# Where list tiles, best entries' rows, the squares of x and the batched heads' selection stand in a fused decoder block

## The chip, the cores and the metric

The kernel runs on one core of one Trainium2 chip. Its time is the device time of one execution, in microseconds (us). The core has five engines that work side by side and each take their own instructions in order: TensorE (PE: matmuls, with its weight loads listed as PEld), VectorE (DVE), ScalarE (ACT), GpSimd (POOL), and SyncE (SP), which here only issues DMA transfers. PE alone has a clock that a throttle grants in part or in full. Transfers between HBM and the on-chip memory run on 16 DMA engines that all queues share.

## The reference

One decoder layer over 1024 tokens of width 1024, all in float32:

```python
h = modulate(rms_norm(x, norm1_w), shift1, scale1)
proj = h @ w_in          # q k v r a_lr su sv g_a g_b
o_gla = rms_norm(gla_chunked(q, k, v, log_a)) * silu(r)
o_sgu = gelu(su) * (W_s @ layer_norm(gelu(sv)) + b)
x = x + gate1 * ((sigmoid(g_a) * o_gla + sigmoid(g_b) * o_sgu) @ w_out)
h2 = modulate(rms_norm(x, norm2_w), shift2, scale2)
x = x + gate2 * peer(h2)
out = rms_norm(x, final_norm_w)
```

`gla_chunked` is gated linear attention with 4 heads. `peer` is a mixer of 16384 one-neuron experts with 8 heads: each token's query of a head is scored against two sets of 128 keys, the 16 best of each set are combined, the 16 best sums name 16 experts, and the output is the sum over heads and experts of softmax weight x gelu(h2 . down[e]) x up[e], where down and up are rows of 1024 numbers. The shifts, scales and gates come from a conditioning vector c.

## The kernel before

**Layout of the work.** The tokens go in two halves of 512 (hf = 0, 1), each of four blocks of 128. For a half the projections are made in weight groups of 512 columns: V0, V1, QK0, QK1, SV0, SV1, R0, R1, A0, A1, SU0, SU1, B0, B1 of w_in, then two passes of w_out, then the four query groups of peer_w_q (w_q; group 0 in two parts of two blocks). A group runs through `stream` (L1264): eight steps k = 0 to 7, one per 128 rows of the weight, each with twelve matmuls of 512 columns into four PSUM accumulators (tag mm, four buffers). Matmuls are made exact by splitting both operands into a high and a low half (fp32r): `weights_ahead` (L1246) loads a weight tile on SP, ACT makes the high half wh (L1253), DVE the low half wl (L1254), three steps ahead, with four tiles staged. After the eighth step the four accumulators are evicted (`evac`), and the next group's first matmul needs the first of them free.

**What runs beside the groups.** At the end of each step `step()` (L1045) pumps generators, which each trace a little more work and yield. A queue has a credit: pump(n) adds n, and one turn is taken for each whole unit. The queues are: qa, the conditioning rows; qr, the routing of the experts; qm, the norms; qf, finishing blocks; qp, the expert stream `peer_stream` (L779); qdir, `direct_rows` (L739). Rates are 1.0 for qr, RP = RP2 = 0.84 for qp (RP3 = 1.3 in the last three query groups of the second half) and RD = 0.62 for qdir.

**Experts.** For each head the best entry (the first of the 16) is known early, by token, and is called a best entry's row: `direct_rows` treats 4 blocks x 8 heads = 32 of them in the second half. For each it gathers 128 rows of down and 128 of up (L752, POOL), takes the dot with h2 on DVE (L764), gelu on ACT (L766), a weight (L767) and adds the up rows times the weight (L773, or L769 on ACT for a block's first head). The gelu is held behind the gates' logarithms (`zlast`). The other entries are packed into list tiles of 128 (token, expert) pairs: `entry_list` (L542) picks indices with a one-hot matmul (L548, L549), gathers both rows at once (L525), `entry_dot` (L572) brings the tokens' h2 rows by matmul into an accumulator (L578, L579), which DVE reads for the dot (L580), or takes gathered h2 rows (L585); the up rows are split (L617 on ACT, L618 on DVE) and added by matmul (L625, L626). List tiles run in the second half from group SV0 on, and then alone after the last query group. Heads that may need more than eight of one key set are batched: `rare` (L390) finds them, gathers their scores (qsc, L428) and selects 16 of each set with `tops16` (L203), then packs them (`pack_rare`). For the first half (gi = 0) it stands in qr after that half's routing, so its turns come in the second half's first groups.

**Order on the engines.** The kernel is written in one program order, but a planner that replays it with its own estimates of durations fixes each engine's order: of the operations that it holds ready, the earlier in the program goes first. Waits between engines are made from the data. `issue_after(ins)` puts an operation behind a given one on the same engine. A generator's place in the program is thus a priority, not a time. On the chip each engine then keeps that order, and an operation that waits holds all behind it.

**The places that the change touches.** `x_prep` (L1170), called after the first half's query group 1 (L1679), loads four tiles of x (xb, tag b4, eight buffers), squares them on ACT with a sum (L1176), makes the reciprocal norms, spreads them over partitions by a matmul (L1165) into an accumulator of the pool aux (two buffers, used by the scores too) and a copy (rrow, L1167), loads xT in four tiles (L1182) and multiplies them (L1184); `h_split` (L1209) later makes hTh and hTl of the second half from it. `ev_qk` (L1366) evicts the QK groups with DVE operations L1382 to L1384 for q and L1399 to L1402 for k. `gla_head` (L1406) runs one head of the attention over four pairs of chunks p, and pumps qdir in each. `w_q` (L1602) evicts a query group on ACT (qt, L1607); `s_part` (L1648) then makes the scores (L1655), copies them (so, L1657) and finds the top 8 (L200, L201).

## Time and profile before

| | |
|---|---|
| median of 3 runs | 1451.9 us (1449.78 to 1454.23) |
| the profiled execution's own time | 1450.17 us |
| its span, first to last instruction | 1448.4 us |
| mean granted PE clock | 0.971 |
| PE busy | 1348.1 us, 93% |
| PE weight loads busy | 1039.6 us, 72% |
| DVE busy | 1091.7 us, 75% |
| ACT busy | 737.9 us, 51% |
| POOL busy | 278.7 us, 19% |
| moved by DMA | 345 MB, mean 238 GB/s |

In the span the first half's groups run from about 34 to 577 us, the second half's from there to about 1245, and the remaining list tiles to the end. A row of a timeline gives start, duration, engine, line, operation, tiles (out<-in), shapes and count, and in brackets the engine's idle time before it with what ended that. A row of waits gives total, count and longest. A row of the chain of waits gives start, duration and what the chain went through. Rows of windows give the stretch, its length and each engine's busy time with its count, then PE's granted clock, the DMA engines' share and GB/s. L12 is line 12 of the kernel.

### The profile page before, as it was taken

Reading aid. Unit: us, or ns where it says so; the run is one execution under the profiler, and the core shown is the slowest. Engines: PE = TensorE matmul, PEld = TensorE weight load, DVE = VectorE, ACT = ScalarE, POOL = GpSimd, SP = SyncE. Lnnn points to the kernel's source line nnn. Section 1 sums busy time; section 2 is a strip of 40 time slices with the busy share of each in tenths; the row PEclk is TensorE's granted clock in tenths of the full one; section 3 lists DMA queues with packets and bytes.
Section 4 is the critical chain, followed back from the end, with each engine's and each line's share of the span. In section 5 each row is a group of like instructions: output and inputs, shape, how many; then the busy total and the mean of one; then the engine's idle time right before and its main releaser. Section 6 shows DMA issues by size and latency. Waiting matters only on the chain.

```text
span 1448.4 us, 19642 instructions
## 1 busy us (share of the span) xinstructions
PE 1348.1 (93%) x6004; PEld 1039.6 (72%) x6004; DVE 1091.7 (75%) x3114; ACT 737.9 (51%) x1611; POOL 278.7 (19%) x275
## 2 busy tenths in 40 slices
PE   3999999999999889997989999999988999789996
PEld 2778877888888778776868787887766886445553
DVE  6584768443468669988879888778889877799775
ACT  4454333333255456474534677556645555556542
POOL 0100001000000011422442133221111024443331
PEclk8899999999999999998999999999998999999999
DMA  9552454322258484757587689796687669987984
GB/s 321 184 214 95 170 184 161 105 95 88 88 171 280 160 291 168 265 177 275 194 308 263 222 325 343 286 354 216 219 324 264 227 216 356 355 347 303 419 331 166
DMA packets 120836, 345.00 MB, mean 238 GB/s; under 512 B 15033, under 2 KB 24505, under 8 KB 108690
## 3 DMA queue, kind: packets, MB, share of 16 engines
q0 software_dynamic: 32064, 165.95, 30.7%
q1 hardware_dynamic: 70992, 133.20, 26.8%
q10 hardware_dynamic: 17666, 44.53, 8.5%
q8 instruction: 48, 0.79, 0.2%
q14 instruction: 66, 0.54, 0.1%
HBM read 319.40 MB, written 24.23 MB: 237 GB/s over the span
## 4 chain that ended last, share of the span: by engine, by line
PE 41%; DMA 8%; DVE 7%; issue 5%; ACT 4%; POOL 1%; ACTq 0%; DVEq 0%; POOLq 0%
PE acc L606 7%; PE mm L181 6%; PE mm L182 6%; PE mm L184 6%; DMA uv<-in_tab_dram,ix 4%; PE mm L187 3%; PE mm L188 3%; PE mm L189 3%; PE aux L1655 2%; PE hps L578 1%; DMA wt<-in_w_inp_dram 1%; PE hps L579 1%; DVE wl L1254 1%; DVE uv L580 1%; DMA xb<-in_x_dram 1%
## 5 line engine op out<-in xcount | busy, mean ns | idle before, releaser
L1253 ACT ACTIVATE wh<-wt 128x512 fp32r<-128x512 f32 x368 | 228.2, 628 | 322.9 <-PE mm L182 133.5
L1254 DVE TENSOR_TENSOR wl<-wt,wh 128x512 fp32r<-128x512 f32 x368 | 247.7, 685 | 137.1 <-ACT wh L1253 73.2
L181 PE MATMUL mm<-wh,hTh 128*128 128x512 f32 x672 | 265.9, 398 | 3.1 <-ACT wh L1253 3.1
L182 PE MATMUL mm<-wh,hTl 128*128 128x512 f32 x672 | 263.8, 395 | 0.0
L184 PE MATMUL mm<-wl,hTh 128*128 128x512 f32 x672 | 207.6, 394 | 0.0
L181 PEld LDWEIGHTS mm<-wh,hTh 128*128 128x128 f32 x672 | 127.1, 189 | 35.0 <-ACT wh L1253 4.8
L182 PEld LDWEIGHTS mm<-wh,hTl 128*128 128x128 f32 x672 | 126.9, 189 | 27.1 <-issue 1.0
L184 PEld LDWEIGHTS mm<-wl,hTh 128*128 128x128 f32 x672 | 125.6, 188 | 27.0 <-DVE wl L1254 0.6
L525 POOL DMA_INDIRECT uv<-in_tab_dram,ix x74 | 80.4, 1086 | 262.9 <-ACT ix L557 178.3
L187 PE MATMUL mm<-wh,hTh 128*128 128x512 f32 x224 | 90.5, 413 | 8.4 <-ACT hTh L1211 5.5
L182 PE MATMUL mm<-hTl,wh 128*128 128x512 f32 x240 | 96.5, 402 | 0.0
L181 PE MATMUL mm<-hTh,wh 128*128 128x512 f32 x240 | 95.9, 400 | 0.0
L580 DVE SCALAR_TENSOR_TENSOR uv<-uv,hps 128x512 f32<-128x512 f32 x112 | 74.8, 679 | 24.5 <-DMA uv<-in_tab_dram,ix 16.8
L188 PE MATMUL mm<-wl,hTh 128*128 128x512 f32 x224 | 89.1, 398 | 0.1
L189 PE MATMUL mm<-wh,hTl 128*128 128x512 f32 x224 | 88.4, 397 | 0.0
L187 PE MATMUL mm<-hTh,wh 128*128 128x256 f32 (+1 forms) x208 | 71.6, 346 | 10.7 <-DVE q L1383 7.6
L188 PE MATMUL mm<-hTl,wh 128*128 128x256 f32 (+1 forms) x208 | 69.8, 337 | 3.0 <-DVE hTl L173 3.0
L184 PE MATMUL mm<-hTh,wl 128*128 128x512 f32 x240 | 71.4, 398 | 0.0
L752 POOL DMA_INDIRECT uvd<-in_down_dram,dix x32 | 37.1, 1159 | 177.8 <-DVE cidx L353 40.0
L618 DVE SCALAR_TENSOR_TENSOR vl<-uv,r,vh 128x512 fp32r<-128x512 f32 x84 | 61.3, 745 | 10.6 <-ACT vh L617 7.7
L189 PE MATMUL mm<-hTh,wl 128*128 128x256 f32 (+1 forms) x208 | 68.9, 337 | 0.0
L578 PE MATMUL hps<-hh,E 128*128 128x512 f32 x132 | 62.4, 473 | 4.5 <-DVE uv L580 3.6
(938 smaller groups left out, 2875.3 us busy)
## 6 DMA issues: line engine op xcount, KB each, us to landing
wt<-in_w_inp_dram SPq DMA_DIRECT2D x224, 256.0 KB, 3.5
wt<-in_w_qp_dram SPq DMA_DIRECT2D x80, 256.0 KB, 3.0
wada<-in_w_ada_dram SPq DMA_DIRECT2D x32, 512.0 KB, 4.8
wt<-in_w_outp_dram SPq DMA_DIRECT2D x64, 256.0 KB, 3.5
wada<-in_w_ada_dram SPq DMA_DIRECT2D x32, 256.0 KB, 5.8
s_d<-so ACTq DMA_DIRECT2D x28, 256.0 KB, 5.3
xr<-in_x_dram ACTq DMA_DIRECT2D x8, 512.0 KB, 6.5
x_d<-x ACTq DMA_DIRECT2D x8, 512.0 KB, 4.4
```

Source lines behind the costliest of these rows:

```text
L181: nc.tensor.matmul(ps, lh, rh, start=False, stop=False)
L182: nc.tensor.matmul(ps, *((lh, rl) if feat else (ll, rh)), start=False, stop=False)
L184: nc.tensor.matmul(ps, *((ll, rh) if feat else (lh, rl)), start=False, stop=False)
L187: nc.tensor.matmul(ps, lh, rh, start=first, stop=False)
L188: nc.tensor.matmul(ps, lh, rl, start=False, stop=False)
L189: return nc.tensor.matmul(ps, ll, rh, start=False, stop=last).ins
L525: nc.gpsimd.indirect_dma_start(out=dst[:], out_offset=None, in_=src, in_offset=off)
L578: nc.tensor.matmul(hps, Ej, hh[:, sl], start=True, stop=False)
L580: nc.vector.scalar_tensor_tensor(uv[0][:, sl], uv[0][:, sl], 1.0, hps, op0=OP.mult, op1=OP.mult, accum_out=r[:, 2 + n:3 + n])
L606: ins = nc.tensor.matmul(acc[:, sl], W, v[:, sl], start=first, stop=last).ins
L1253: nc.scalar.activation(wh, wt, AF.Identity)
L1254: nc.vector.tensor_tensor(wl, wt, wh.bitcast(F32), op=OP.subtract)
```

## The change

Three edits. First, `step` takes the step's number k and pumps qp and qdir only in steps 0 to 5, at 4/3 of their rates; in `gla_head`, qdir is pumped with 2 x RD at p = 0 and 1 in place of RD at each of the four. Second, `x_prep` is cut in two: `x_load` issues the four loads of x after query group 1 as before, and the rest follows after query group 2, with the squares placed behind the last eviction of that group's qt on ACT (`last_qt`); the loads of xT move with the rest, behind one more group of weights on SP. Third, `rare` takes no turn past its gather until the second half's QK0 eviction code exists (`crit`, the last operation of head 1's k); for group 0 its `tops16` are placed behind that operation on DVE. For group 1 nothing changes there.

```diff
@@ -387,6 +387,8 @@
         nc.vector.tensor_copy(tsel[:, :, c0:c0 + 2 * K1], w[:, :, 0].rearrange("p (b k) -> p b k", b=BH))
         yield
 
+    crit = []
+
     def rare(gi, rps):
         nb = len(GROUPS[gi])
         n, col = nb * PH, NBLK + NG + gi
@@ -429,10 +431,13 @@
                                      in_=s_g[gi].rearrange("b p (h k) -> (b p h) k", h=PH),
                                      in_offset=bass.IndirectOffsetOnAxis(ap=ix, axis=0))
         yield
+        while not crit:
+            yield
         tv = r2.tile([P, 1, 2, TOPK], F32, name="qtv")
         ti = r2.tile([P, 1, 2, TOPK], U32, name="qti")
-        for c in range(2):
-            tops16(tv[:, 0, c], ti[:, 0, c], sc[:, c])
+        with nullcontext() if gi else tc.issue_after(crit[0]):
+            for c in range(2):
+                tops16(tv[:, 0, c], ti[:, 0, c], sc[:, c])
         yield
         ts, sel = yield from select16(r2, tv, ti, 1, "q")
         tsel = r2.tile([P, 3 * TOPK + 2], F32, name="qtsel")
@@ -1042,13 +1047,14 @@
     qa, qr, qp, qdir, qm, qf = Queue(), Queue(), Queue(), Queue(), Queue(), Queue()
     rate = {"a": 1.0, "r": RA, "d": RD, "p": RP, "m": 1.0}
 
-    def step():
+    def step(k):
         qa.pump(rate["a"])
         qr.pump(rate["r"])
         qm.pump(rate["m"])
         qf.pump()
-        qp.pump(rate["p"])
-        qdir.pump(rate["d"])
+        if k < 6:
+            qp.pump(rate["p"] * 4 / 3)
+            qdir.pump(rate["d"] * 4 / 3)
 
     with ExitStack() as pa:
         wst_p = pa.enter_context(tc.tile_pool(name="wstage", bufs=WT))
@@ -1167,13 +1173,20 @@
             nc.scalar.activation(rrow, rps, AF.Identity)
             return rrow
 
-        def x_prep(t0):
-            ss = sm_p.tile([P, BH], F32, name="ss")
+        def x_load(t0):
+            xbs = []
             for i in range(BH):
                 xb = t4("xb")
                 with tc.issue_after(last_wt[0]):
                     nc.sync.dma_start(xb, x[t0 + i * P:t0 + (i + 1) * P, :])
-                nc.scalar.activation(xb, xb, AF.Square, accum_out=ss[:, i:i + 1])
+                xbs.append(xb)
+            return xbs
+
+        def x_prep(t0, xbs):
+            ss = sm_p.tile([P, BH], F32, name="ss")
+            for i, xb in enumerate(xbs):
+                with tc.issue_after(last_qt[0]):
+                    nc.scalar.activation(xb, xb, AF.Square, accum_out=ss[:, i:i + 1])
             rrow = rstd_row(ss, nc.vector)
             xts = []
             for k in range(0, KD, 2):
@@ -1237,7 +1250,7 @@
             at.append(a)
 
         order_ = (G_V0, G_V1, G_QK0, G_QK1, G_SV0, G_SV1, G_R0, G_R1, G_A0, G_A1, G_SU0, G_SU1, G_B0, G_B1)
-        plan, made, last_wt = [], [], []
+        plan, made, last_wt, last_qt = [], [], [], []
         for _ in range(NHALF):
             plan += [(w_inp[g], k) for g in order_ for k in range(KD)]
             plan += [(w_outp[m], k) for _ in range(2) for k in range(KD) for m in range(2)]
@@ -1271,7 +1284,7 @@
                     body(k, ws, pss)
                     if post and k in post:
                         post[k]()
-                    step()
+                    step(k)
                 for i in range(npsum):
                     evac(i, pss[i])
 
@@ -1399,7 +1412,9 @@
                         nc.vector.tensor_tensor(kk[:, :, 0:3:2], p4, v4c(eGi), op=OP.mult)
                         nc.vector.tensor_tensor(kk[:, :, 1], p4[:, :, 0], d4[:, :, 0], op=OP.mult)
                         nc.vector.tensor_tensor(k4[:, :, 1], p4[:, :, 1], d4[:, :, 1], op=OP.mult)
-                        nc.vector.tensor_tensor(k4[:, :, 0], kk[:, :, 1], last(1), op=OP.mult)
+                        kl = nc.vector.tensor_tensor(k4[:, :, 0], kk[:, :, 1], last(1), op=OP.mult)
+                        if hf and not crit and h % 2:
+                            crit.append(kl.ins)
                         qk[h] += [kk, kt]
                 return f
 
@@ -1418,7 +1433,8 @@
                 nc.vector.copy_predicated(a, amask.unsqueeze(1).to_broadcast([P, 4, P]), aps_)
                 hc = slice(h * DV, (h + 1) * DV)
                 for p in range(4):
-                    qdir.pump(RD)
+                    if p < 2:
+                        qdir.pump(2 * RD)
                     s_in, s_out = S[h][p % 2], S[h][1 - p % 2]
                     sps = auxt([P, DV])
                     nc.tensor.matmul(sps, ktok[:, p], vt[p][:, hc], start=True, stop=True)
@@ -1604,7 +1620,7 @@
                 if half is None:
                     def ev(m, ps):
                         qts[m] = t2("qt")
-                        nc.scalar.activation(qts[m], ps, AF.Identity)
+                        last_qt[:] = [nc.scalar.activation(qts[m], ps, AF.Identity).ins]
 
                     group(w_qp[q], ev, True)
                 else:
@@ -1677,7 +1693,9 @@
                     rate["p"] = RP3
                 w_q(q)
                 if hf == 0 and q == 1:
-                    xts = x_prep(HALF)
+                    xbs = x_load(HALF)
+                if hf == 0 and q == 2:
+                    xts = x_prep(HALF, xbs)
             qa.drain()
     behind.append(last_s[0])
     use.append(peer_pools("1", "left", UVC, 1, 2, AH, EB, True))
```

## The prediction

> **What bounds the kernel now.** I read the page's engine totals first, then the span cut into stretches at the group boundaries, then TensorE's waits, then the chain of waits and the timelines around the three longest of them.
>
> ```profile
> span 1448.4 us, 19642 instructions
> PE 1348.1 (93%) x6004; PEld 1039.6 (72%) x6004; DVE 1091.7 (75%) x3114; ACT 737.9 (51%) x1611; POOL 278.7 (19%) x275
> ```
>
> TensorE (PE) is busy for 93% of the span, so the change can only win back idle time of PE and slow-clock time that follows it. The stretches below show where these are (us; busy time of PE, its weight loads, VectorE, ScalarE, GpSimd; then PE's granted clock, the share of the DMA engines, GB/s).
>
> ```profile
> 500.00:525.00 25.00, 20.75 (x92) 17.08 (x92) 16.05 (x83) 15.25 (x27) 5.67 (x5) 0.91 0.79 291
> ...
> 550.00:600.00 50.00, 50.00 (x254) 41.59 (x253) 49.73 (x220) 31.29 (x53) 4.82 (x4) 1.00 0.55 187
> ...
> 657.60:665.70 8.10, 0.52 (x4) 0.13 (x2) 8.03 (x23) 2.82 (x7) 2.87 (x2) 0.69 1.02 400
> 665.70:701.00 35.30, 34.57 (x161) 28.59 (x161) 31.21 (x103) 22.10 (x44) 4.97 (x5) 0.93 0.59 199
> ...
> 748.00:1007.00 259.00, 255.10 (x1156) 207.82 (x1156) 215.90 (x542) 159.77 (x364) 68.32 (x62) 1.00 0.80 290
> 1007.00:1024.60 17.60, 12.54 (x58) 8.84 (x57) 15.61 (x39) 14.23 (x31) 2.41 (x2) 0.90 0.60 213
> 1024.60:1142.00 117.40, 107.47 (x543) 86.30 (x543) 101.24 (x249) 66.87 (x143) 15.39 (x16) 0.94 0.78 273
> 1142.00:1245.00 103.00, 101.22 (x451) 76.65 (x451) 78.64 (x333) 56.88 (x124) 31.46 (x30) 1.00 0.74 273
> ```
>
> The reader should see three things. The ten groups SV0 to B1 of the second half (748 to 1007) leave PE idle for only 259.0 - 255.1 = 3.9 us. The transition from QK0 to QK1 (657.6 to 665.7) leaves it idle for 7.6 us, with VectorE (DVE) busy for 8.03 of 8.10 us. And 550 to 600, where the second half's activations are made, has no idle PE but a DVE that is full. PE's waits name what ended each of these:
>
> ```profile
> PE mm L187 <- DVE q L1383: 7.6, 1, 7.6
> ...
> PE gaux L1426 <- DVE rdr L767: 4.5, 1, 4.5
> PE tps L548 <- DVE uv L580: 4.5, 3, 3.2
> ...
> PE aux L1655 <- ACT qt L1607: 4.2, 1, 4.2
> ...
> PE hps L578 <- DVE uv L580: 3.6, 5, 2.2
> ```
>
> Nothing here is removed from the program, so PE's, DVE's and ScalarE's (ACT's) totals stay; what moves is the order on in-order engines.
>
> **The squares of x (x_load, x_prep).** Today four squares stand on ACT ahead of the evictions of query group 1, and each waits for its load:
>
> ```profile
> 508.96 11.75 DMA xb<-in_x_dram
> ...
> 524.16 0.43 PE mm L187
> ...
> 527.58 0.27 PE mm L184
> ...
> 528.29 0.23 PE mm L187
> ```
>
> ```profile
> 520.74 1.06 ACT L1176 ACTIVATE xb<-xb 128x1024 f32<-128x1024 f32 x1 [1.42 <-DMA xb<-in_x_dram]
> ...
> 522.31 2.04 ACT L1607 ACTIVATE qt<-mm 128x512 f32<-128x512 f32 x4
> ```
>
> PE waits 4.2 us for qt, and its next matmuls come at 0.43 us each until 527.6, against 0.23 afterwards: 4.6 us (522.9 to 527.6) at half pace, 2.2 us lost. With the squares bound behind the evictions of query group 2 the loads have landed a group earlier, so both go: -6.4 us. Not all of it stays, because the row of reciprocal norms, the eight products with xT and the split of h for the second half now start a group later (the xT loads too, on SP behind one more group of weights, 2 MB in place of 4 MB in one burst):
>
> ```profile
> 544.00 1.02 PE L1165 MATMUL aux<-dg,ones 128*128 128x512 f32 x2
> ...
> 576.88 0.40 PE L187 MATMUL gaux<-hTh,walr_h 128*16 128x512 f32 x1
> ...
> 579.55 0.48 PE L187 MATMUL mm<-wh,hTh 128*128 128x512 f32 x1
> ```
>
> ```profile
> 537.53 0.60 ACT L1657 ACTIVATE so<-aux 128x512 f32<-128x512 f32 x1 [0.50 <-PE aux L1655]
> ...
> 564.20 0.58 ACT L1657 ACTIVATE so<-aux 128x512 f32<-128x512 f32 x1
> ```
>
> ```profile
> 545.70 5.03 DVE L1184 TENSOR_TENSOR xt<-xt,rrow 128x512 f32<-128x512 f32 x8 [0.24 <-ACT rrow L1167]
> ```
>
> The broadcast matmul (L1165) shares its two accumulators with the score tiles. It came at 544.0, 6.5 us after the last score eviction of query group 1 (537.5); the same distance after that of group 2 (564.2) is 570.7. One more 1.7 us to the first product (544.0 to 545.7) and 5.0 us of products put the split at 572.4 to 577.4, where PE reads it first at 576.9 and for V0 at 579.6. The cover is gone: what hid the products was a whole query group, and now it is 2 to 4 us on a DVE that is busy for 49.7 of 50. The bounds are 0 (the planner brings L1165 forward, since the group's scores are ready in any order) and +5.0 (all eight products stand in front of V0). I take +1.5, as the first k-slice needs only one product. Net -4.9.
>
> **Batched heads' selection (rare, group 0).** Its first operation waits on DVE for a gather, just ahead of QK0's evictions:
>
> ```profile
> 657.10 0.49 DVE L204 MAX8 qtv<-qsc 128x8 f32<-128x128 f32 x2 [3.19 <-DMA qsc<-s_d,qix]
> ...
> 658.28 1.28 DVE L773 SCALAR_TENSOR_TENSOR yd<-uvd,rdr,yd 128x1024 f32<-128x1024 f32 x1
> ...
> 663.62 1.22 DVE L764 SCALAR_TENSOR_TENSOR uvd<-uvd,h2d 128x1024 f32<-128x1024 f32 x1
> ...
> 664.77 0.42 DVE L1382 SCALAR_TENSOR_TENSOR qs<-mm,eG 128x256 f32<-128x256 f32 x1
> ```
>
> ```profile
> 657.01 0.63 ACT L1253 ACTIVATE wh<-wt 128x512 fp32r<-128x512 f32 x1 [4.86 <-DMA wt<-in_w_inp_dram]
> ```
>
> The present price of the transition is 7.6 us of idle PE and (1 - 0.93) x 35.3 = 2.5 us of slow clock behind it: 10.1. Taking the selection out does not free 3.2 us, since the next operation in DVE's queue is a low half (wl) whose weight tile was split at 657.0 to 657.6 anyway. What it frees is the selection's own operations ahead of 664.8, some 2 us (0.49 for two maxima, and as many more index, replace and sum operations). The rest of the queue there is best entries' rows (L764, L773), about 1.2 us each, four of them from 658.3 to 664.8. They are the second part of the same knot.
>
> **Best entries' rows in six steps (qdir, gla_head).** Rates are 4/3 in six of eight steps, and 2 x RD in two of a head's four, so totals are unchanged (8 x 0.62 = 6 x 0.827). By program order two steps' rows (1.24) now come before QK0's last two steps, so one or two fewer stand ahead of its evictions: 2.4 us each with dot and sum. But a row is paced by its gather, not by its place in the program:
>
> ```profile
> DMA to landing us min/median/max: 4.1/6.3/11.2
> ```
>
> I take -4 for the whole transition (2 us of selection, one row's dot, one us of clock), between 0 (the rows land no sooner, and stand where they stood) and -10.1 (no wait left, as at the 748 to 1007 boundaries). The selection itself reappears behind QK0, at QK1's boundary, with its own waits; the peer stream that needs it starts only after QK1's heads, near 748.
>
> Slow clock follows short waits too; the stretch to 475 holds this one, and its clock is below full:
>
> ```profile
> PE aux L1655 <- ACT qt L1623: 2.1, 1, 2.1
> ```
>
> ```profile
> 450.00:475.00 25.00, 22.66 (x150) 20.74 (x149) 21.63 (x34) 13.94 (x24) 1.06 (x2) 0.96 0.73 249
> ```
>
> I therefore leave 1.5 us of slow clock in the count. [...]
>
> The same rows delay head 3 at 745, with PE waiting 4.5 us:
>
> ```profile
> 743.36 1.23 DVE L764 SCALAR_TENSOR_TENSOR uvd<-uvd,h2d 128x1024 f32<-128x1024 f32 x1 [2.26 <-DMA uvd<-in_down_dram,dix]
> ...
> 744.51 0.72 DVE L1418 COPY_PREDICATED at<-amask,gaux 128x512 f32<-128x512 int32 x1
> ```
>
> DVE stands before a dot whose gather has not landed, and the head's mask (L1418) stands behind it. Packing two pumps into p = 0 and 1 keeps a row at the head's start. I take -1, between -4.5 and +4.5 (a second head caught likewise).
>
> **List tiles in six steps (qp).** From 748 to 1007 there are 3.9 us to win. Against it: DVE carries 21.6 us in a group of 25.9, of which the low halves take 8 x 0.685 = 5.5.
>
> ```profile
> L1254 DVE TENSOR_TENSOR wl<-wt,wh 128x512 fp32r<-128x512 f32 x368 | 247.7, 685 | 137.1 <-ACT wh L1253 73.2 <-PE mm L184 60.4 <-ACT r L590 1.1
> ```
>
> If all the other 16.1 us had to fit in six steps of 3.24 us beside six low halves (4.1), that is 20.2 in 19.4: at worst 0.8 us over in each group. Against that, the evictions at the end find a free queue. I take 0 there, between -3.9 and +8. From 1007 to 1142, evictions of B1 and of w_out mix with list work, PE idles 5.1 + 9.9 = 15.0 us and the clock is at 0.90 and 0.94. Two steps without list work help exactly there: -1.5, between -8 (half of the idle) and +5.6 (seven streams at 0.8). From 1142 on PE idles 1.8 us of 103 and I count nothing.
>
> Gathers packed tighter also meet the weight loads, which sit on PE's path through wh:
>
> ```profile
> 647.91 8.99 DMA wt<-in_w_inp_dram
> ```
>
> ```profile
> wt<-in_w_inp_dram SPq DMA_DIRECT2D x224, 256.0 KB, 3.5
> ```
>
> A load's median is 3.5 us and the worst piece on the chain 9.0, against about three steps of lookahead.
>
> [...]
>
> **Sum.** -4.9 - 4 - 1 + 0 - 1.5 = -11.4 us on the profiled execution's 1450.17 us (1448.4 of span and 1.8 around it): 1438.8. That execution lies 1.7 us under the median of the runs shown, 1451.9, so the prediction is 1440 us. All best ends give 34 us less, all worst 17 us more.
>
> **Rivals.** (a) Only the squares pay: rows still land when they land, and the planner leaves the same ones ahead of QK0's evictions. For it: the gather waits above. Against it: the pin behind the last eviction holds the selection. 1451.9 - 4.9 = 1447. (b) Slower: DVE cannot carry list work in six steps, PE's list matmuls (L548, L578) wait for L580's reads of their accumulator, and 17 streams of the second half that pump lists pay 0.8 us: 13.6 - 4.9 = +8.7, 1460. It decides once those two waits, 4.5 + 3.6 = 8.1 us now, exceed about 13. For it: DVE at 83% from 748 to 1007. Against it: two steps later the queue catches up. (c) The change does not do what it says: the planner fills engines by its own times whatever the place in the program, and V0's late split eats the squares: 1451. (d) All three knots go and B1's boundary too: -6.4 - 10.1 - 4.5 - 4 = -25, 1427.
>
> **Chances.** Forecast 0.52 (its own range 1433 to 1447), (a) 0.17, (b) 0.17, (c) 0.08, (d) 0.06. A measurement tells about 0.3%, 4.4 us, from no change, so faster means below 1447.5. The forecast, (d) and half of (a) are faster: 0.66. Half of (a) and most of (c): 0.16 the same. (b) and the rest: 0.18 slower. The range 1428 to 1454 leaves out most of (b) and (d).
>
> **What would show it.** Right: no wait of L1655 for qt L1607 near 518; the wait of L187 for L1383 under 5 us; qsc's selection after L1402; L1165 within 8 us of its scores; L548 and L578 waits still near 8 us. Wrong: a PE wait at V0 (L187 on hTl or xt) over 5 us; a new wait of over 5 us at QK1 or its heads; PE idle from 748 to 1007 above 10 us.

## The result

The change makes the kernel slower. Its median is 1467.1 us (six executions, 1460.4 to 1475.7) against 1452.0 for the kernel before in the same session, a ratio of 1.0114 with a 95% interval of 1.0086 to 1.0142. The forecast was 1440 and the range ended at 1454: the sign is wrong. The profiled execution of the changed kernel took 1465.8 us. One execution, the profiled one of the kernel x1r below, was disturbed (1917 us) and stands in no other number here. In the changed kernel's lines the score matmul is L1671 (was L1655), the query eviction L1623 (L1607), hTl L1229 (L1216), q L1396 (L1383), the best entry's dot L769 (L764), the list dot L585 (L580), and the final rows' sum L704 (L699).

The engine totals of the page after:

```profile
span 1464.1 us, 19671 instructions
...
PE 1348.8 (92%) x6004; PEld 1040.1 (71%) x6004; DVE 1092.9 (75%) x3114; ACT 738.3 (50%) x1615; POOL 294.4 (20%) x275
```

PE's busy time is nearly what it was (1348.1); 15.0 of the 15.7 us of longer span are idle PE. Its waits over the whole span (total, count, longest):

```profile
PE aux L1671 <- ACT qt L1623: 8.8, 4, 3.2
PE acc L630 <- DVE fin L704: 6.8, 1, 6.8
...
PE mm L187 <- DVE q L1396: 5.2, 1, 5.2
...
PE gaux L1442 <- DVE at L1433: 4.5, 2, 2.3
...
PE mm L189 <- DVE hTl L1229: 3.6, 1, 3.6
```

The forecast's targets did shrink: q at QK1 from 7.6 to 5.2, and head 3 waits 2.3 (one of the two of L1442) in place of 4.5. But the query evictions, which were to vanish from it (4.2), cost 8.8 in four places, the row of hTl is new, and that of fin was 0.5.

To see where the time went, I compare when each group's first matmul starts in the two traces. The stage from query group 1 of the first half to V0 of the second takes 7.6 us more, and the one from SV1 to B1 takes 14.9 more; V1 to SV0 takes 6.2 less. (The nine groups from 748 on are SV1 to B1; the prediction called them SV0 to B1.) The two long stages before (columns as in the prediction: stretch, length, busy PE, PEld, DVE, ACT, POOL, granted clock, DMA share, GB/s):

```profile
495.00:607.80 112.80, 108.55 (x524) 88.83 (x524) 93.87 (x430) 64.59 (x111) 20.62 (x18) 0.97 0.63 218
...
748.70:1024.60 275.90, 266.93 (x1212) 216.15 (x1211) 230.81 (x580) 173.30 (x391) 70.46 (x63) 0.99 0.78 284
```

And after:

```profile
494.20:614.70 120.50, 110.92 (x525) 89.07 (x524) 95.48 (x432) 61.76 (x109) 24.71 (x19) 0.97 0.59 206
...
749.40:1040.10 290.70, 270.88 (x1213) 219.17 (x1212) 229.52 (x577) 174.85 (x396) 70.13 (x62) 0.97 0.75 267
```

With the same matmuls, the first stage has 9.6 us of idle PE in place of 4.2 and 2.4 more of busy PE; the second 19.8 in place of 9.0 and 3.9 more of busy PE at a clock of 0.97.

**What came of the squares.** Four loads of xT now leave SP in the middle of query group 2, ahead of weight tiles (timeline of SP after):

```profile
522.97 10.76 SPq L1263 DMA_DIRECT2D wt<-in_w_qp_dram  x4
533.78 2.95 SPq L1195 DMA_DIRECT2D xt<-in_xT_dram  x4
537.35 14.82 SPq L1263 DMA_DIRECT2D wt<-in_w_qp_dram  x5
```

The timeline of ACT after, at that group's end:

```profile
543.41 1.96 ACT L1623 ACTIVATE qt<-mm 128x512 f32<-128x512 f32 x3 [0.95 <-PE mm L189]
550.47 0.63 ACT L1266 ACTIVATE wh<-wt 128x512 fp32r<-128x512 f32 x1 [5.09 <-DMA wt<-in_w_qp_dram]
...
552.51 0.58 ACT L1623 ACTIVATE qt<-mm 128x512 f32<-128x512 f32 x1
552.99 1.05 ACT L1189 ACTIVATE xb<-xb 128x1024 f32<-128x1024 f32 x1
```

Three evictions are done by 545.4. Then ACT stands 5.1 us before a high half. High halves are made in the order of the weight loads, and this one's tile is the first behind the xT loads on SP, the one issued at 537.35: its high half starts 13.1 us later, with 2 MB of xT ahead of it in the queue and four gathers issued from 537.3 to 541.2. (The profile page of the kernel before gives these tiles a median of 3.0 us from issue to landing.) The fourth eviction stands behind that high half, and PE waits 3.2 us for it. The squares come only behind that eviction, 32 us later than before. In x_only and the three nudged versions of the change below, which have the same late loads, ACT stands 1.8 to 5.4 us before the tile in the same place, 11.2 to 13.4 us after its issue. The timeline of DVE after, through the second half's activations:

```profile
570.73 4.90 DVE L1197 TENSOR_TENSOR xt<-xt,rrow 128x512 f32<-128x512 f32 x8
...
579.75 1.22 DVE L769 SCALAR_TENSOR_TENSOR uvd<-uvd,h2d 128x1024 f32<-128x1024 f32 x1
...
583.96 1.23 DVE L769 SCALAR_TENSOR_TENSOR uvd<-uvd,h2d 128x1024 f32<-128x1024 f32 x1 [2.52 <-DMA uvd<-in_down_dram,dix]
...
586.91 2.50 DVE L1229 TENSOR_TENSOR hTl<-xt,hTh 128x512 fp32r<-128x512 f32 x4
...
593.02 1.88 DVE L1229 TENSOR_TENSOR hTl<-xt,hTh 128x512 fp32r<-128x512 f32 x3
```

The products are done by 575.6, as forecast (577.4). The low halves are not: two best entries' dots stand in front of them, the second with 2.5 us of waiting for its gather. The last low half ends at 594.9, against 586.6 before, V0 has begun at 578.5, and PE waits 3.6 us for one.

### The profile page after: what moved, and what is told of

It is laid out like the page before. It is cut to its first block, busy times and chain, and to the rows that moved or that the text cites. A ratio compares the mean times of both kernels' runs of the same rounds, so it can differ in the third digit from the quotient of the medians.

```text
span 1464.1 us, 19671 instructions
## 1 busy us (share of the span) xinstructions
PE 1348.8 (92%) x6004; PEld 1040.1 (71%) x6004; DVE 1092.9 (75%) x3114; ACT 738.3 (50%) x1615; POOL 294.4 (20%) x275
## 4 chain that ended last, share of the span: by engine, by line
PE 24%; issue 10%; DVE 8%; DMA 8%; ACT 4%; POOL 2%; ACTq 0%; DVEq 0%; POOLq 0%
PE acc L611 6%; PE mm L181 3%; PE mm L182 3%; PE mm L184 2%; DMA uv<-in_tab_dram,ix 2%; PE mm L188 1%; PE mm L189 1%; PE mm L187 1%; PE hps L583 1%; PE hps L584 1%; DVE wl L1267 1%; DMA wt<-in_w_inp_dram 1%; POOL uv L530 1%; PE acc L631 1%; PE acc L630 1%
## 5 line engine op out<-in xcount | busy, mean ns | idle before, releaser
L585 DVE SCALAR_TENSOR_TENSOR uv<-uv,hps 128x512 f32<-128x512 f32 x112 | 75.1, 683 | 20.2 <-PE hps L584 10.7
L611 PE MATMUL acc<-uv,W 128*128 128x512 f32 x128 | 61.4, 602 | 5.1 <-ACT W L600 3.8
```

What stands on the lines that cost most here:

```text
L585: nc.vector.scalar_tensor_tensor(uv[0][:, sl], uv[0][:, sl], 1.0, hps, op0=OP.mult, op1=OP.mult, accum_out=r[:, 2 + n:3 + n])
L611: ins = nc.tensor.matmul(acc[:, sl], W, v[:, sl], start=first, stop=last).ins
```

## The experiments

Every kernel was timed against the kernel before, which had medians of 1451.9, 1451.7, 1449.4, 1451.7 and 1449.0 in the five sessions. The columns in the middle are stages of one profiled execution of each, less the same stage of the kernel before, from the starts of the groups' first matmuls: I, query group 1 to V0 (495 to 608); II, V1 to SV0 (608 to 749); III, SV1 to B1 (749 to 1025); IV, w_out and query group 0 of the second half (1025 to 1143); V, the rest. What comes ahead of I, -4.5 to +3.8 us with no pattern by edit, and a profiled execution up to 7 us off its kernel's median, are why stages and medians do not add up exactly. The stages of x1r are those of x1r_again, the same kernel. In the column of squares, late means behind the last eviction of query group 2, own group behind that of query group 1. x_only, n_rd, a_rp83 and a_rp85 had only four executions, the change and x2e six, the others 10 to 12.

| kernel | squares | lists | rows | selection | median us | ratio (95%) | I | II | III | IV | V |
|---|---|---|---|---|---|---|---|---|---|---|---|
| the change (after) | late | yes | yes | yes | 1467.1 | 1.0114 (1.0086-1.0142) | +7.6 | -6.2 | +14.9 | +2.0 | -1.9 |
| x_only | late | - | - | - | 1471.8 | 1.0106 (1.0033-1.0179) | +10.2 | +0.5 | +0.1 | +6.5 | +3.6 |
| l_only | - | yes | - | - | 1455.8 | 1.0032 (1.0000-1.0064) | +1.2 | +3.8 | -2.7 | +5.9 | -4.0 |
| d_only | - | - | yes | - | 1459.9 | 1.0053 (1.0020-1.0085) | +1.5 | +1.8 | +9.9 | -1.0 | -0.9 |
| r_only | - | - | - | yes | 1451.1 | 0.9983 (0.9952-1.0015) | +2.9 | -2.6 | +5.7 | -2.3 | 0.0 |
| x1 | own group | - | - | - | 1458.7 | 1.0045 (1.0018-1.0071) | -2.1 | +2.8 | +4.4 | +6.5 | +1.9 |
| x2e | late, xT early | - | - | - | 1463.1 | 1.0085 (1.0052-1.0118) | +1.1 | +0.2 | -0.8 | +6.2 | +3.6 |
| ld | - | yes | yes | - | 1460.2 | 1.0050 (1.0017-1.0082) | +3.0 | +2.2 | +9.5 | -1.1 | -2.9 |
| ldr | - | yes | yes | yes | 1458.4 | 1.0039 (1.0011-1.0067) | -0.8 | -2.3 | +12.9 | +0.4 | -2.5 |
| after_x1 | own group | yes | yes | yes | 1460.9 | 1.0078 (1.0051-1.0105) | -1.1 | +2.9 | +12.4 | +3.2 | -2.5 |
| x1r | own group | - | - | yes | 1445.8 | 0.9965 (0.9939-0.9992) | | | | | |
| x1r_again | own group | - | - | yes | 1445.7 | 0.9960 (0.9934-0.9986) | -1.2 | +1.3 | -1.3 | -5.0 | +3.5 |
| x1r_rp85 | own group | - | - | yes | 1442.2 | 0.9951 (0.9923-0.9979) | -2.0 | +0.8 | +0.4 | -6.2 | -0.3 |
| n_rd | - | - | 0.63 | - | 1467.3 | 1.0132 (1.0052-1.0211) | +0.2 | +2.7 | +5.6 | +11.0 | -0.1 |
| n_rp2 | - | 0.83 | - | - | 1448.9 | 0.9990 (0.9966-1.0015) | -2.8 | +1.6 | +1.9 | +2.0 | +1.0 |
| n_rp | - | 0.85 | - | - | 1449.7 | 0.9984 (0.9953-1.0016) | +2.5 | +0.7 | -1.3 | -4.9 | +4.1 |
| a_rd63 | late | yes | yes, 0.63 | yes | 1456.4 | 1.0023 (0.9995-1.0052) | +8.7 | -7.9 | +7.1 | +2.3 | -3.7 |
| a_rp83 | late | yes, 0.83 | yes | yes | 1467.7 | 1.0129 (1.0080-1.0178) | +6.4 | -5.5 | +16.7 | -5.1 | +8.3 |
| a_rp85 | late | yes, 0.85 | yes | yes | 1465.9 | 1.0118 (1.0066-1.0169) | +7.6 | -5.6 | +12.5 | -5.3 | -1.5 |

### One part alone (x_only, l_only, d_only, r_only)

x_only takes the change's x_load, x_prep and last_qt, r_only its crit in rare and ev_qk, both word for word:

```diff
# x_only
-                    xts = x_prep(HALF)
+                    xbs = x_load(HALF)
+                if hf == 0 and q == 2:
+                    xts = x_prep(HALF, xbs)
...
# r_only
+        while not crit:
+            yield
...
+        with nullcontext() if gi else tc.issue_after(crit[0]):
...
# l_only
-        qp.pump(rate["p"])
+        if k < 6:
+            qp.pump(rate["p"] * 4 / 3)
# d_only
-        qdir.pump(rate["d"])
+        if k < 6:
+            qdir.pump(rate["d"] * 4 / 3)
...
-                    qdir.pump(RD)
+                    if p < 2:
+                        qdir.pump(2 * RD)
```

> Only the squares move (x_load after query group 1, x_prep after query group 2); list tiles, rows and the batched heads stay as before. Theory 1 (the places in the traces add up): the changed kernel is 5.7 us ahead of the kernel before when query group 2 starts and 6.9 us behind when V1 of the second half starts, so this edit alone is worth about +7 us, 1459, with PE waiting 3 to 5 us for hTl in V0 and for qt in query group 3. Rival (order noise: any edit makes the planner lay out the second half anew, and the losses sit wherever that falls): no tie to V0; the time lies anywhere within 1440 to 1470, and V0's wait is small. A second rival, my forecast: -5 us, 1447.

> Only the expert stream qp is pumped in steps 0 to 5 at 4/3; the rows (qdir), the squares and the batched heads stay as before. Theory 1: the changed kernel loses 20.6 us between SV0 and SU1 of the second half and wins some 4.5 back at the end of B1, so this edit alone is worth +10 to +16 us, 1462 to 1468, with PE waits of over 10 us between SV0 and SU1. Rival (order noise): the loss is not there, or falls elsewhere. My forecast: within -3 to 0.

> Only the best entries' rows (qdir) are pumped in steps 0 to 5 at 4/3, and with 2 x RD at two of four p in a head. Theory 1: the changed kernel wins 2.3 us from QK0 to QK1 and 2.8 us from QK1's heads to SV0; rows and batched heads share these, so -2 to -4 us, 1448 to 1450. Rival (order noise): a loss or gain of 5 us or more with no tie to QK0 and the heads.

> Only the batched heads' selection of group 0 moves behind QK0's evictions. Theory 1: the wait of PE for q at QK1's start falls from 7.6 us to about 5, -2 to -3 us, 1449. Rival (order noise): a loss or gain of 5 us or more, elsewhere than from QK0 to SV0.

The squares alone lose in stage I what the whole change loses there and more, and about as much in all (ratio 1.0106 against 1.0114). Lists alone lose about 4 us, with an interval that reaches down to nothing, and none of it in stage III, where Theory 1 put their price. Rows alone, which Theory 1 let gain, lose 9.9 us in just that stage. So Theory 1 had the places right and one owner wrong. Of its four totals only that of r_only came within 3 us; x_only is 13 us above its own. And the selection alone brings the wait for q at QK1 from 7.6 to 6.6, not to 5.

### Which half of the late squares (x2e, x1)

x2e leaves the xT loads behind the x loads, a group ahead of the late squares. x1 leaves all of x_prep in its old place and only pins the squares:

```diff
# x1, against the kernel before, with the change's x_load and last_qt
-                nc.scalar.activation(xb, xb, AF.Square, accum_out=ss[:, i:i + 1])
...
+            for i, xb in enumerate(xbs):
+                with tc.issue_after(last_qt[0]):
+                    nc.scalar.activation(xb, xb, AF.Square, accum_out=ss[:, i:i + 1])
...
-                    xts = x_prep(HALF)
+                    xts = x_prep(HALF, x_load(HALF))
# x2e, in x_load behind the loads of x (moved from x_prep)
+            xtl = []
+            for k in range(0, KD, 2):
+                xt = v4.tile([P, 2, HALF], F32, name="xt", tag="v4")
+                with tc.issue_after(last_wt[0]):
+                    nc.sync.dma_start(xt, xT[k * P:(k + 2) * P, t0:t0 + HALF].rearrange("(a p) t -> p a t", p=P))
...
```

> The kernel before with the squares behind query group 2's last eviction, as in the change, but with the four xT loads left where they were, one group earlier, right behind the x loads. Theory 2 splits the loss of the late squares into two parts: the xT loads of 2 MB at 539 to 548 us, under which the weight loads take 7 us, so that ScalarE waits 5.4 us for a weight tile that stands ahead of the last query eviction; and the late split of h. Here the first part is gone and the second stays: no such wait of over 2 us at the end of query group 2 (near 553 to 558), V0 still waits 3 to 4 us for the low half of h and its group ends 8 to 9 us later than it began to be ahead; time 1456 to 1460, some 12 less than with late loads. Rival: the late xT loads are what made V0 late: then V0 starts and ends on time, and the time is that of the early squares, 1447. Own forecast of the first prediction: 1447 to 1450, the late split costing 1.5.

> The kernel before, with one edit: the four squares of x are pinned behind the last eviction of query group 1, the group in which their loads land, instead of standing ahead of its evictions; loads of x and xT, the row of reciprocal norms, the products and the split stay in the program where they were. Theory 2 (late by a group): what cost the change its gain at the squares is that they came 32 us later (553 instead of 521 us) and that the xT loads moved in among the weight loads of the next boundary. Both are absent here, so the 5 us at query group 1 stay won: group starts from query group 2 to V1 lie 4 to 6 us ahead of the kernel before, no wait of the score matmul for a query eviction over 2 us at 524 or 553, none of V0's matmul for the low half of h, and the time is 1447 (1444 to 1450). Rival A (the stall moves): the weight tiles of query group 2 land near 526 as before, and PE, 5 us earlier, now waits for those: 1451 to 1452. Rival B (any other order loses, by some 8 to 15 us, wherever it is disturbed): above 1456, with the loss spread over places that have nothing to do with x.

The timeline of ACT in x2e, at query group 2's end:

```profile
539.19 1.56 ACT L1619 ACTIVATE qt<-mm 128x512 f32<-128x512 f32 x3
540.62 0.64 ACT L1265 ACTIVATE wh<-wt 128x512 fp32r<-128x512 f32 x1
...
542.69 0.58 ACT L1619 ACTIVATE qt<-mm 128x512 f32<-128x512 f32 x1
```

The same high half stands between the third and the fourth eviction, and waits for nothing. Stage I is 9 us shorter than in x_only: 2.3 of it in query group 2, 3.5 in query group 3, where this wait was, and 3.3 in V0, whose wait for the low half of h fell from 3.8 to 1.7. (The expectation had V0's wait stay; a wait of 3.0 for a query eviction came at query group 3's end instead.) So in stage I the place of the xT loads is the larger half of the loss. In the whole time the two kernels are not told apart: medians 8.7 us from each other in different sessions, ratios of 1.0085 and 1.0106 with intervals that overlap. The smaller half is the late squares themselves: x1, with both in place, is 3.2 us shorter still in stage I. Yet x1 keeps only 2.1 of the 4.9 us that it gains by the start of query group 2. PE's longest wait in the stage, and ACT's timeline:

```profile
PE aux L1662 <- ACT so L1664: 2.7, 1, 2.7
```

```profile
546.63 0.20 ACT L766 ACTIVATE rdr<-rdr 128x1 f32<-128x1 f32 x1 [2.92 <-DVE uvd L764]
552.85 0.20 ACT L766 ACTIVATE rdr<-rdr 128x1 f32<-128x1 f32 x1 [6.02 <-DVE uvd L764]
...
554.53 1.06 ACT L1664 ACTIVATE so<-aux 128x512 f32<-128x512 f32 x2
```

PE, now ahead, meets the copies of the scores behind a best entry's gelu, which waits 6 us for its dot; that is one part of what query group 3 loses. And x1 as a whole is 7 us slower than before, most of it in stages III and IV, which it does not touch. Its Rival B (any other order loses) had foretold that total, and is tried by itself in the nudges below.

### Lists, rows and selection together (ld, ldr, after_x1)

ld joins the edits of l_only and d_only, ldr adds that of r_only. after_x1 is the changed kernel with x1's place for the squares:

```diff
# after_x1, against the change
                 if hf == 0 and q == 1:
-                    xbs = x_load(HALF)
-                if hf == 0 and q == 2:
-                    xts = x_prep(HALF, xbs)
+                    xts = x_prep(HALF, x_load(HALF))
```

> The kernel before with list tiles and best entries' rows in six of eight steps (and rows in two of a head's four), without the edits of squares and selection. Alone the first cost 4 us and the second 8. If places add up (Theory 1): 1464, with the half-clock pieces at 808 and 876 that the rows alone showed, and 10 to 13 us lost between SV0 and SU1 (749 to 940). If the two collide, since both fill the same six steps: 20 us lost there, as in the changed kernel, and 1470 or more. If the 20 us of the changed kernel come from the selection's new place or from the late squares: under 5 us lost there, and 1452 to 1458.

> The changed kernel without its edit of the squares: lists and rows in six steps, and the selection behind the last product of a head. By adding up the single parts (4 + 8 - 1): 1463. If the squares' edit is worth the 20 us here that it showed alone: 1447. Theory 1 says that the loss from 749 to 940 us belongs to these parts and stays at 16 to 20 us, with PE waiting for the final rows (L704's sum) near 932: then 1458 to 1466, since the gains of QK0 to QK1 (2 us) and of the heads (3 us) stay too. Rival (order): the loss moves to other places, and the wait for the final rows is not among them.

> The changed kernel with only its squares mended: they are pinned behind the evictions of query group 1, where their loads land, and the xT loads, norms and products are back in their old place; lists, rows and selection stay as in the change. If the parts add up, the mending gives what it gave alone, 1471.8 - 1458.7 = 13 us: 1454. If the late squares no longer matter beside the loss from 749 to 940 us (later stretches take up the slack, as the kernel with lists, rows and selection alone, 1458, suggests): 1458 to 1462, 5 to 9 us less. Order theory: anywhere from 1455 to 1467.

Stage III costs 9.5 to 12.9 us in all three, as it did in d_only (9.9), which has neither lists, selection nor squares. The stretch SV1 to B1 of d_only, and of l_only beside it:

```profile
754.40:1040.10 285.70, 272.00 (x1210) 220.26 (x1208) 229.16 (x573) 175.22 (x392) 70.68 (x62) 0.96 0.75 267
```

```profile
756.70:1029.90 273.20, 265.61 (x1212) 216.23 (x1212) 231.41 (x580) 173.79 (x393) 69.83 (x63) 0.99 0.80 286
```

13.7 us of idle PE against 7.6, and 6.4 us more of busy PE at a lower clock (0.96 against 0.99). No single wait explains d_only: the longest is 2.5 (matmul of a list tile for vh). In ldr, after_x1 and the changed kernel PE also waits for the final rows' sum (fin): 2.5, 3.2 and 6.8 us, 0.5 in the kernel before and nothing in d_only. The sum waits on DVE for a load (after, then before):

```profile
DVE fin L704 <- DMA fin<-y_d: 7.2, 1, 7.2
```

```profile
DVE fin L699 <- DMA fin<-y_d: 3.3, 1, 3.3
```

The load takes 11 us in both (issued 919.97, landed 931.2; 903.79 and 914.86), but the sum now stands in DVE's queue 3.9 us earlier against it, ahead of what PE's list matmuls need.

The rows themselves cannot be what is in the way through most of that stage: the last best entry's row ends 15 to 32 us after SV1's start in every one of these kernels but x1 (34). What differs later is which list step falls on which group. The list matmuls L625 per group from R0 to SU1 number 2, 8, 6, 9, 7, 10 in the kernel before, and the same in n_rp2, n_rp and l_only; 3, 7, 6, 10, 6, 9 in d_only and ld; 3, 6, 7, 10, 8, 8 in the change. But other kernels that lose less there have other counts too: 2, 6, 8, 8, 6, 10 in x_only (+0.1), 4, 7, 7, 8, 7, 10 in r_only (+5.7) and x1r_again (-1.3). Nor is the list stream simply late: the first of these matmuls comes 44 us after SV1's start in the kernel before, 46 in d_only, 43 in the change and 50 in ldr. So it is shown that rows in six steps cost stage III; by which path they do is not shown, and stays open.

### The size of a change of order as such (n_rd, n_rp2, n_rp, a_rd63, a_rp83, a_rp85)

One constant each, which adds no work, no wait and no transfer:

```diff
-RD = 0.62
+RD = 0.63          # n_rd on the kernel before, a_rd63 on the change
-RP = .84
+RP = .83           # n_rp2 on the kernel before, a_rp83 on the change; .85 in n_rp, a_rp85
```

> The kernel before with best entries' rows pumped at 0.63 per step in place of 0.62, and nothing else: no work, wait or transfer is added, and it serves as the size of what a change of order as such costs. Order theory (the eight-microsecond loss of the kernel with the squares just behind their own group's evictions is what any disturbance of this order costs): 1455 to 1460, with the loss in places that differ from one kernel to the next. Theory 2 (losses belong to what was moved): 1450 to 1454, within the measurement of the kernel before.

> The kernel before with list tiles pumped at 0.83 per step in place of 0.84, and nothing else; the second size of a change of order as such. Order theory: 1455 to 1460. Theory 2: 1450 to 1454.

> The kernel before with the rate of list tiles 0.85 in place of 0.84. Draw theory: a third draw around the kernel before; of the two so far one cost nothing and one 18 us, so 1450 to 1467, and not faster than the kernel before by over 4 us if that is one of the best of its neighbours. Place theory: 1450 to 1454.

> The changed kernel with the rate of best entries' rows 0.63 in place of 0.62 and nothing else. The same nudge cost the kernel before 18 us (1467 against 1449). Draw theory (what the change lost is largely the draw of a new order, and its parts have small prices of their own): this kernel comes out at another time altogether, anywhere from 1448 to 1470, and with the other nudges of the changed kernel spreads by more than 10 us. Place theory (the loss belongs to what was moved: squares a group late, rows and selection behind SV1): the waits at V0 for the low half of h and at the end of query group 2 for a query eviction stay, and the time is 1460 to 1475.

> The changed kernel with the rate of list tiles 0.83 in place of 0.84 and nothing else; in the kernel before this nudge cost nothing. Draw theory: 1448 to 1470, another time than the changed kernel's 1467 by more than 4 us. Place theory: 1462 to 1472 with the same waits at the same groups.

> The changed kernel with the rate of list tiles 0.85 in place of 0.84, the third nudge of it. From the query group that starts at 495 to the group V1, the changed kernel and its two nudges lose 6.4 to 8.7 us against the kernel before, all with the same waits (score matmul for a query eviction, V0 for the low half of h); that place's price should be 6 to 9 here too. The stretch from SV0 to SU1 cost 18, 6 and 18 us in the three: by the draw theory this one is again anything from 3 to 18, and the time 1452 to 1470.

One nudge of the rows' rate, by 1.6%, costs the kernel before 18 us (by its four executions; the interval goes from 8 to 31) and gains the change 11. Four nudges of the list rate move the time by 3 us at most. Neither theory stands whole. Against the pure draw: stage I costs 6.4 to 8.7 us in the change and in all three of its nudges, and 10.2 in x_only, each with waits for query evictions (5.1 to 7.7 us in sum) and for the low half of h (1.9 to 3.8), though in the two nudges of the list rate the query wait at query group 2's end gives way to one at group 3's; stage III costs 12.5 to 16.7 in three of the four and 7.1 in the fourth. Against pure places: n_rd loses about as much as the whole change with nothing edited but a rate.

### A version that beats both (x1r, x1r_again, x1r_rp85)

x1r and x1r_again join the edits of x1 and r_only; x1r_rp85 is the same with one more:

```diff
-RP = .84
+RP = .85
```

> The kernel before with the squares behind query group 1's own evictions and the selection behind the last product of a head, the two parts that did best alone. By adding up: 1458.7 - 0.7 = 1458. It beats the kernel before (under 1447) only if the 7 us that the squares lost in later stretches were a matter of the order those stretches happened to take, which the selection's new place reshuffles again; order theory: 1450 to 1460.

> The kernel before with the squares behind query group 1's own evictions and the selection behind the last product of a head, run again for a narrower interval and a second profile: 1443 to 1449 if its 3.6 us gain holds. In the profile: no wait for a query eviction over 2 us at the ends of query groups 1 and 2, and, if the gain is the parts' own, a wait of QK1's first matmul for q shorter than 7.6; if it is a draw, the gain lies in stretches that neither part touches.

> The version that beat the kernel before by 6 us (squares behind their own group's evictions, selection behind the last product of a head), with the rate of list tiles 0.85 in place of 0.84. In its profile the gain lies in the second half's w_out groups (1055 to 1143 us), which neither part touches. Draw theory: with this nudge that gain goes or another comes, 1447 to 1462; only 1 to 2 us, at the end of query group 1 up to V1, stay. If the gain is the parts' own: 1443 to 1449.

x1r is 3.6 and 6.0 us faster than the kernel before in two sessions, and x1r_rp85 6.7, each with an interval under 1. The gain survives the nudge, so it does not hang on that one rate. But it is not where the edits are, except for 1 to 2 us in stage I. It lies in w_out's second pass and query group 0 (before, then x1r_rp85, then n_rd, which lost there):

```profile
1055.10:1142.80 87.70, 77.77 (x417) 62.56 (x416) 76.99 (x187) 48.88 (x104) 10.85 (x12) 0.92 0.82 292
```

```profile
1052.70:1134.50 81.80, 73.81 (x417) 61.15 (x416) 75.01 (x182) 47.10 (x102) 12.53 (x13) 0.98 0.87 308
```

```profile
1062.90:1161.70 98.80, 83.20 (x428) 66.38 (x429) 84.26 (x206) 51.93 (x116) 16.40 (x14) 0.90 0.76 270
```

For the same 417 matmuls, PE's busy time is 4 us less (clock 0.98 against 0.92) and its idle time 1.9 less. Over the whole of stage IV, x1 alone has +6.5 and r_only -2.3; together they have -5.0 and -6.2. Why the two together reach this order stays open.

## Why the prediction was wrong

Three sums show where the forecast of -11.4 parts from the traces. The squares with V0's late split were to give -4.9; stage I gave +7.6. QK0 to the heads was to give -5; stage II gave -6.2. Lists were to give -1.5 and rows nothing beyond QK0 and the heads; stages III and IV gave +16.9.

**The squares, -6.4.** Right in kind: at query group 1's end the wait fell from 4.2 to 1.8, and query group 2 starts 5.0 us earlier against query group 1. What is left is again a high half, waiting ahead of the fourth eviction for the weight tile that is first behind the four x loads (issued at 508.56, high half at 521.58).

**V0's late split, +1.5 within 0 to +5.** This is the term that was mis-sized first: the loss of stage I behind those 5.0 us is 7.6 + 5.0 = 12.6, against bounds of 0 and 5. Two things were missed. The prediction looked at DVE's own eight products and found them in time, which they were; it left out that DVE is in order, with two best entries' dots (1.2 us each) and a gather's wait (2.5 us) between products and low halves. And it counted the xT loads' move as "2 MB in place of 4 MB in one burst", a relief; it did not ask which weight tile stands behind them on SP, and which eviction behind that tile's high half on ACT. x2e shows that this move, which had no price, is worth 9 us of x_only's loss in the stage.

**QK0 to QK1, -4, and head 3, -1.** The size was about right, the cause only in part. The wait fell from 7.6 to 5.2, and the selection now starts at 682, behind head 1's k. But moving it accounts for little: the wait is 4.9 to 7.2 in the eleven kernels whose selection stands behind QK0's evictions, 6.2 to 8.2 in the eight where it stands ahead, and r_only's is 6.6. In x_only the planner put the selection there by itself (683), with a wait of 5.0. As the prediction feared, the rows did not move: four dots and four sums still stand on DVE from 654 to 669, ahead of QK0's evictions, which was the premise of rival (a). The wait at head 3 shrinks with rows in six steps (1.9 in d_only, 3.9 in r_only), though with x1's squares too (2.3). With the heads, stage II gives 6.2 of the expected 5. Part of it is paid for by stage I, though: ldr, without the late squares, gives 2.3, and after_x1 loses 2.9.

**Lists, 0 and -1.5.** The bounds nearly held: l_only has -2.7 in stage III, within -3.9 to +8, and +5.9 in stage IV, just past the end of -8 to +5.6; in sum on the bad side. One reading behind them was off: 748 to 1007 holds nine groups, not ten, so a group is 28.8 us with 24.0 of DVE, and the same working gives 1.0 us over in each in place of 0.8. (All best ends add up to 33 us less, not 34.)

**Rows.** The largest failure. The prediction priced them at QK0 and at head 3, and put them at nothing in the groups behind, without a reason. Stage III cost 14.9 us, and 9.9 with the rows' edit alone. All eight kernels with rows in six steps lose 7 to 17 us in stage III; the eleven others, with the kernel before, lie between -2.7 and +5.7. (One trace each; between the two groups lie only 1.4 us.) The path from the rows to this loss stays open.

**Rivals.** (b) had the sign, not the cause: the waits of list matmuls for the list dot were to exceed 13 us and fell, from 8.1 to 2.2. (c) was half right: squares and selection are where the edits put them, so the planner did not undo those, but V0's late split did eat the squares, as (c) also said. **The signs to look for** did their work: PE idle from 748 to 1007 above 10 was named as proof against the forecast, and came, at 16.2; the limit for a wait at V0 (5 us) was too high, at 3.6 and a granted clock of 0.50 behind it (588.7 to 592.1 us).

**The chances.** No rival said that an order is one among many whose times spread by more than 1%. Some 18 us for a nudge of 1.6% is more than the whole effect that was forecast, though the other nudge of the kernel before, up and down, moved it by 2 us at most; a chance of .18 for slower was too small for a change that reorders the whole second half.

## What to carry to other kernels

When work is moved on in-order queues, follow its loads too: which transfer stands behind them, which operation waits for that one, and who stands behind that operation (here a weight tile, a high half that waited 5.1 us on ACT, and a query eviction that PE waited 3.2 us for). Where a planner or rates fix a long order, first nudge a rate that adds no work, up and down, to learn how far the time moves by itself; an edit's worth is then read in its own stage, over several such orders, not from one total. A gain or a loss that lies in stages which no edit touches (x1, x1r) belongs to the new order, and says little about the edit.

## What the runs showed of the hardware

In the changed kernel's trace slow clock came behind waits that were short one by one, and not behind every longer one. Rows of windows, 3.4 us each:

```profile
663.80:667.20 3.40, 1.47 (x7) 0.89 (x5) 2.54 (x6) 0.63 (x1) 2.79 (x3) 1.00 1.02 405
667.20:670.60 3.40, 0.09 (x1) 0.12 (x2) 3.40 (x9) 0.95 (x4) 1.92 (x2) 1.00 1.04 404
...
865.20:868.60 3.40, 1.71 (x7) 0.83 (x5) 2.84 (x8) 2.38 (x6) 1.35 (x1) 1.00 1.02 425
868.60:872.00 3.40, 2.96 (x7) 2.38 (x8) 2.98 (x6) 3.37 (x8) 0.00 (x0) 0.50 0.80 314
872.00:875.40 3.40, 3.40 (x17) 2.81 (x17) 3.11 (x8) 3.34 (x8) 1.88 (x2) 1.00 0.36 105
...
1213.30:1216.70 3.40, 1.71 (x4) 0.40 (x3) 1.84 (x3) 0.00 (x0) 2.00 (x2) 1.00 1.04 424
1216.70:1220.10 3.40, 2.31 (x12) 2.00 (x13) 1.93 (x3) 2.92 (x8) 1.53 (x2) 1.00 1.00 404
```

From 865.2 to 868.6 us no wait is over 1.2 us, PE is idle for 1.7 in all, and the clock in the row from 868.6 to 872.0 was 0.50. A single wait of 2.8 us (1215.0 to 1217.8) leaves 1.7 and 1.1 us of idle PE in its two rows; the clock was 1.00 in both, and still 1.00 from 1220.1 to 1223.5. It was also 1.00 from 667.2 to 670.6, behind 1.9 us of idle PE in the row to 667.2, and 0.50 from 670.6 to 674.0, behind 3.3 us. So in this trace the price of a wait could not be told from its length alone: 1.7 us for the slow row (3.4 us at 0.50), or nothing. What decides between the two is not shown.
